# Norms of the gated heads: folding the squares to 64 rows, and one product with ones in place of two

## The chip, the cores and the metric

The kernel runs on one core of one Trainium2 chip. The metric is the device time of one execution in microseconds; lower is better. A run's time is given as the median of several executions, and one execution was recorded by the hardware profiler.

## The reference

One layer of a hybrid decoder trunk, sequence 1024, width 1024, all in float32. Its input is normalized and projected by one wide matrix (7184 columns). Eight heads of differential softmax attention and four heads of gated linear attention (GLA, value width 256) run beside each other, each head's output is normalized and gated, and both are projected back. What matters here is the norm of the gated heads:

```python
def rms_norm(x, g):
    xf = x.astype(jnp.float32)
    y = xf * lax.rsqrt(jnp.mean(xf * xf, axis=-1, keepdims=True) + NORM_EPS)
    return (y * g.astype(jnp.float32)).astype(x.dtype)
...
    ob = gla_chunked(...)                  # (B, S, 4 heads, 256)
    ob = rms_norm(ob, gla_g).astype(x.dtype)
    ob = ob.reshape(B, S, GLA_WIDTH) * jax.nn.silu(gb)
```

So for every position and head, 256 squares have to be summed.

## The kernel before

**Number format.** Products run on TensorE in a reduced form of float32. A value is split into a high part (a rounding copy on ScalarE, `act.copy` into an `F32R` tile) and a low part (value minus high part, a subtraction on VectorE), and three of the four cross products are summed. Line 117, the helper `mm`, issues every matmul, and line 120 (`tr`) every transpose. Both are kept in the order in which the program gives them; the instructions of the other engines, and SP's DMAs, are put in order by a planner that estimates when each would be ready (some are pinned, too).

**The projection.** The wide product is made by a scheme of seven products of half blocks (Strassen's kind) for each pair of 128-column blocks. The list `order` has 196 steps `(pair, n)`. A step is 12 matmuls of 512 columns, or 24 of 256 for most pairs, on results `x`, `y`, `z` in PSUM. `go(n)` runs steps. Before a step, `prepare` makes the weights of that and the three following steps: raw weights (`w_raw`, loaded at line 194), sums of them on VectorE (line 296), high part on ScalarE (315), low part on VectorE (316), in a ring of five tiles. Finished sums (`c`, lines 411 and 440) leave through SP's queue to DRAM, to be loaded again by the heads. For the attention values (kind `VA`, steps 97 to 141 in part) a step `n = 7` takes three tiles of the ring `c`.

**The ring `c`.** `t_c(name)` takes a tile of a ring of four (128 rows, 512 floats). The copies `s` of some steps, the sums `c`, the output weights' high parts `wo_hi`, and the norms' `sq` and `r` all come from it. A tile whose content is stored becomes free when the store has landed.

**The gated heads.** `gla(g)` is a generator; each `yield` ends one portion. The four heads run in a chain, `fill`, of which `go` takes one portion after each projection step from step 86 on:

```python
    go(order.index((12, 5)) - made[0])
    fill.append(chain(*(gla(g) for g in range(GLA_HEADS))))
    go(len(order) - made[0] - LEAD)
    for _ in fill[0] if fill else ():
        pass
```

With `LEAD = 8` there are 102 such steps (86 to 187); what is left of the chain after them would run by itself. A head has two halves of 512 positions. In one half: the loads; `pa` and `pk` (scores in the chunk and transposed keys; GpSimd masks the scores, line 775); `kv` (state updates, `gu` on VectorE); `gpo` (outputs, copied to `go`, the tile `o`); then the norm (lines 826 to 859). The value width of 256 lies in two parts of 128 rows. ScalarE squares both (`sqs`), VectorE adds them (`sq`), and the sum over the 128 rows is a product with a matrix of ones: one matmul with the high part and one with the low part of `sq` (`gms`). Ln and Exp on ScalarE give `r`, then VectorE scales and gates `o`, and high and low parts are stored to `mixe` (line 856). A half takes 11 portions, and three steps lie between the squares and the product.

The attention heads' norms (`attn_norm`, lines 1126 to 1138) sum 128 rows; there the squares are folded to 64 rows, and high and low part share one tile of 128 rows and one product.

**What comes behind.** After step 187 the queries and keys of the first attention head are loaded (`load_qk`, lines 875 and 878) into buffers that the gated heads used: `ks` goes into the tags `ks0` and `ks1`, in which `o` and the gates lie. The scores (`sc`) begin after the last step, with the output product (`ypart`) beside them.

Of the kernel before, what the change touches and what calls it, by code (L numbers as in the profile page):

```python
# [9 lines left out]
F32R = mybir.dt.float32r  # L10
AF = mybir.ActivationFunctionType
ALU = mybir.AluOpType
PSUM = bass.MemoryType.PSUM

P = 128
# [16 lines left out]
def hymba_kernel(  # L32
# [21 lines left out]
    act, dve, pool, pe, sp = nc.scalar, nc.vector, nc.gpsimd, nc.tensor, nc.sync  # L54

    def fp(t):
        return t.bitcast(F32)
# [11 lines left out]
    ones = const.tile([P, P], F32R, name="ones")  # L69
# [40 lines left out]
    def take_bank(shape, name):  # L110
        i = free.pop(0)
        return bank(i, shape, name), i
# [3 lines left out]
    def mm(*a, **k):  # L116
        tc.keep_in_program_order(pe.matmul(*a, **k))  # L117
# [35 lines left out]
    kp = ctx.enter_context(tc.tile_pool(name="kp", bufs=1))  # L153
# [3 lines left out]
    def t2k(tag, bufs, name, dt=F32, shape=(P, 512)):  # L157
        return ap.tile(list(shape), dt, tag=tag, name=name, bufs=bufs)

    def t_c(name, dt=F32):  # L160
        return t2k("c", 4, name, dt)
# [55 lines left out]
    i = order.index((1, 4))  # L217
# [540 lines left out]
    def gla(g):  # L758

        u = None  # L760
        for half in range(2):
# [48 lines left out]
            for m in range(2):  # L810
                po, ib = take_bank([P, 2, 256], "gpo")
                for i in range(2):
                    c = slice((2 * m + i) * P, (2 * m + i + 1) * P)
                    for t in range(2):
# [3 lines left out]
                            start=True, stop=(us[2 * m + i] is None),  # L818
# [9 lines left out]
            sqs = kp.tile([P, 2, 512], F32, tag="k1", name="sqs")  # L828
            for t in range(2):
                act.activation(sqs[:, t], o[:, t], AF.Square)  # L830
            sq = t_c("sq")
            dve.tensor_tensor(sq, sqs[:, 0], sqs[:, 1], ALU.add)
            hl = kp.tile([P, 2, 512], F32R, tag="k1", name="sq_hl")
            act.copy(hl[:, 0], sq)
            dve.tensor_tensor(hl[:, 1], sq, fp(hl[:, 0]), ALU.subtract)
            yield
            yield
            yield
            ms, ib = take_bank([P, 512], "gms")
            for i in range(2):  # L840
                mm(ms, ones, hl[:, i], start=(i == 0), stop=(i == 1))
            r = t_c("r")
            act.activation(r, ms, AF.Ln, bias=eps_t, scale=1.0 / 256)
            free.append(ib)
# [39 lines left out]
# [5 lines that stand above are left out]
# [636 lines left out]
```

## Time and profile before

| what | value |
|---|---|
| time, median of 3 runs | 982.13 us (981.99 to 982.59) |
| profiled execution, its own time | 980.34 us |
| its span, first to last instruction | 978.6 us |
| granted TensorE clock, mean | 0.999 |
| instructions | 15745 |
| projection steps with gated heads beside them | about 278 to 590 us |

A row of the profile names the line, engine, operation, the tile written `<-` the tiles read, the size, and how often it ran. PE is TensorE's matmuls, PEld its weight loads, DVE VectorE, ACT ScalarE, POOL GpSimd, SPq the queue from which SP issues DMAs. Brackets at the end of a row of the timeline hold the time that the engine had been idle before it, and what ended that. A matmul's duration is its latency: successive matmuls overlap, so the distance between starts is what one costs.

### The profile page before, as it was taken

How to read it: one execution, taken by the hardware profiler on the slowest of the kernel's cores; microseconds unless marked ns; L12 is line 12 of the kernel's file. 1: busy time of each engine (PE TensorE's matmuls, PEld its weight loads, DVE VectorE, ACT ScalarE, POOL GpSimd, SP SyncE). 2: the span in 40 equal slices, each digit the busy share in tenths (PEclk: the TensorE clock that was granted, in tenths of full speed). 3: DMA queues.
4: the chain of work that ended last, by engine and by line, in shares of the span. 5: the costliest groups of instructions: out<-in, count | busy, mean ns of one | idle time of the engine just before them, and what ended most of it. 6: DMA issues, size and time to landing. Idle time of an engine off the chain costs nothing.

```text
span 978.6 us, 15745 instructions
## 1 busy us (share of the span) xinstructions
PE 956.6 (98%) x5338; PEld 829.7 (85%) x5338; DVE 736.0 (75%) x1452; ACT 600.9 (61%) x1164; POOL 135.3 (14%) x142
## 2 busy tenths in 40 slices
PE   6999999999999999999999999999999999999997
PEld 5998988888889998899888888878888888888785
DVE  6986597798766677586786876487888888898554
ACT  8642365486467445445566765366777687887773
POOL 4300000000000010000100100021322222443322
PEclk9999999999999999999999999999999999999999
DMA  9443456646765858897988866997657669994777
GB/s 353 143 123 93 124 148 202 229 169 233 253 234 168 266 183 276 247 299 230 298 254 255 270 191 217 357 300 250 206 173 234 233 202 351 351 283 107 151 209 146
DMA packets 152593, 220.45 MB, mean 225 GB/s; under 512 B 17104, under 2 KB 83664, under 8 KB 152416
## 3 DMA queue, kind: packets, MB, share of 16 engines
q1 hardware_dynamic: 148480, 212.10, 66.5%
q0 software_dynamic: 4032, 7.34, 4.8%
q8 instruction: 42, 0.69, 0.3%
q14 instruction: 39, 0.32, 0.1%
HBM read 133.93 MB, written 88.60 MB: 227 GB/s over the span
## 4 chain that ended last, share of the span: by engine, by line
PE 87%; DMA 4%; DVE 4%; ACT 2%; issue 1%; SPq 1%; POOL 0%; DVEq 0%; ACTq 0%; POOLq 0%
PE x L117 21%; PE y L117 14%; PE z L117 14%; PE ypart L117 13%; PE sc L117 7%; PE po L117 5%; PE yps L117 4%; PE wtr L120 3%; PE gpo L117 2%; DMA ks<-k_d 1%; PE kv L117 1%; DMA wo_raw<-in_w_out_dram 1%; DMA w_raw<-in_w_in_dram 1%; PE gkl_ps L117 1%; DVE w L316 1%
## 5 line engine op out<-in xcount | busy, mean ns | idle before, releaser
L315 ACT CAST w<-w_raw 128x512 fp32r<-128x512 f32 (+1 forms) x164 | 112.4, 688 | 97.2 <-PE y L117 46.2
L316 DVE TENSOR_TENSOR w<-w_raw,w 128x512 fp32r<-128x512 f32 (+1 forms) x164 | 126.5, 773 | 52.1 <-ACT w L315 45.6
L1048 ACT ACTIVATE p<-p,stt 128x896 f32<-128x896 f32 (+7 forms) x128 | 99.3, 777 | 37.7 <-DVE stt L1038 33.6
L427 ACT COPY s<-x 128x512 f32<-128x512 f32 x84 | 49.1, 585 | 86.9 <-PE x L117 83.9
L1054 POOL TENSOR_SCALAR p<-p,stt,lam 128x1024 f32<-128x1024 f32 (+3 forms) x64 | 56.2, 877 | 226.2 <-DVE stt L1053 223.8
L296 DVE TENSOR_TENSOR w_raw<-w_raw 128x512 f32<-128x512 f32 (+1 forms) x96 | 75.8, 790 | 15.4 <-DMA w_raw<-in_w_in_dram 14.1
L1038 DVE CUSTOM_DVE_ANT_0 p<-sc,maskt 128x512 f32<-128x512 f32 (+3 forms) x128 | 74.3, 585 | 14.9 <-PE sc L117 13.8
L775 POOL TENSOR_SCALAR_AFFINE_SELECT gan<-gan 128x512 f32<-128x512 f32 x8 | 17.6, 2198 | 486.3 <-ACT gan L774 486.3
L117 PE MATMUL ypart<-wo_hi,m_hi 128*128 128x512 f32 x192 | 79.6, 414 | 0.1
L117 PE MATMUL y<-h_hi,w 128*128 128x512 f32 x320 | 79.6, 391 | 0.0
L117 PE MATMUL z<-s_hi,w 128*128 128x512 f32 x320 | 79.6, 391 | 0.0
L117 PE MATMUL x<-s_hi,w 128*128 128x512 f32 x320 | 79.6, 391 | 0.0
L117 PE MATMUL ypart<-wo_hi,m_lo 128*128 128x512 f32 x192 | 75.5, 393 | 0.0
L117 PE MATMUL ypart<-wo_lo,m_hi 128*128 128x512 f32 x192 | 75.4, 393 | 0.0
L117 PE MATMUL sc<-k,q 128*128 128x512 f32 (+1 forms) x192 | 69.0, 363 | 1.2 <-DVE stt L1038 1.2
L117 PEld LDWEIGHTS x<-s_hi,w 128*128 128x128 f32 x320 | 59.7, 188 | 12.2
L117 PEld LDWEIGHTS y<-h_hi,w 128*128 128x128 f32 x320 | 59.6, 188 | 12.2
L117 PEld LDWEIGHTS z<-s_hi,w 128*128 128x128 f32 x320 | 59.5, 188 | 12.0
L117 PE MATMUL sc<-ks,q 128*128 128x512 f32 (+1 forms) x192 | 66.1, 347 | 1.0 <-DMA ks<-k_d 1.0
L1096 ACT CAST wt_hi<-wtr 128x512 fp32r<-128x512 f32 (+1 forms) x80 | 42.8, 535 | 25.3 <-PE wtr L120 24.5
L1097 DVE TENSOR_TENSOR wt_lo<-wtr,wt_hi 128x512 fp32r<-128x512 f32 (+1 forms) x80 | 50.6, 633 | 9.1 <-ACT wt_hi L1096 8.5
L1057 DVE SCALAR_TENSOR_TENSOR p<-p,stt,p 128x1024 f32<-128x1024 f32 (+3 forms) x64 | 52.1, 814 | 4.1 <-POOL p L1054 3.9
(224 smaller groups left out, 2237.3 us busy)
## 6 DMA issues: line engine op xcount, KB each, us to landing
w_raw<-in_w_in_dram SPq DMA_DIRECT2D x56, 512.0 KB, 4.5
wo_raw<-in_w_out_dram SPq DMA_DIRECT2D x32, 256.0 KB, 2.8
wo_d<-wo_hi SPq DMA_DIRECT2D x32, 256.0 KB, 2.9
wo_d<-wo_raw SPq DMA_DIRECT2D x32, 256.0 KB, 3.3
q<-q_d SPq DMA_DIRECT2D x32, 256.0 KB, 4.6
k<-k_d SPq DMA_DIRECT2D x32, 256.0 KB, 5.3
ks<-k_d SPq DMA_DIRECT2D x64, 128.0 KB, 6.5
wo_hi<-wo_d SPq DMA_DIRECT2D x16, 512.0 KB, 6.4
```

Source lines behind the costliest of these rows:

```text
L117: tc.keep_in_program_order(pe.matmul(*a, **k))
L120: tc.keep_in_program_order(pe.transpose(dst, src, ident))
L296: dve.tensor_tensor(dst, a, b, ALU.subtract)
L315: act.copy(w[0], src)
L316: dve.tensor_tensor(w[1], src, fp(w[0]), ALU.subtract)
L427: act.copy(b[k], ps)
L1038: ins = dve.tensor_tensor_reduce(p[:, a:e], sc[:, : e - a], maskt[:, NZ + P - (e - a) :] if last else maskt[:, : e - a], 1.0, 3e38 if i == ...
L1048: act.activation(p[:, :n], p[:, :n], AF.Exp, bias=st[:, m : m + 1], scale=-1.0, accum_out=st[:, 2 + m : 3 + m],)
L1054: pool.tensor_scalar(p1[:, :n], p1[:, :n], st[:, 5:6], lam, ALU.mult, ALU.mult)
L1057: dve.scalar_tensor_tensor(p0[:, :n], p0[:, :n], st[:, 4:5], p1[:, :n], ALU.mult, ALU.subtract)
L1096: act.copy(hi[:, :n], pt[:, :n])
L1097: dve.tensor_tensor(lo[:, :n], pt[:, :n], fp(hi[:, :n]), ALU.subtract)
```

## The change

The two parts' squares are added as before, but for rows 0 to 63 and rows 64 to 127 separately (`sq` and `fold`, both in rows 0 to 63 of a tile of the ring `c`), and a third addition folds the two into 64 rows. The high part of these goes into rows 0 to 63 of `sq_hl` and the low part into rows 64 to 127, so that one product with ones sums both. One `yield` more stands between the squares and the product, so a half takes 12 portions.

```diff
             sqs = kp.tile([P, 2, 512], F32, tag="k1", name="sqs")
             for t in range(2):
                 act.activation(sqs[:, t], o[:, t], AF.Square)
-            sq = t_c("sq")
-            dve.tensor_tensor(sq, sqs[:, 0], sqs[:, 1], ALU.add)
-            hl = kp.tile([P, 2, 512], F32R, tag="k1", name="sq_hl")
-            act.copy(hl[:, 0], sq)
-            dve.tensor_tensor(hl[:, 1], sq, fp(hl[:, 0]), ALU.subtract)
+            sq, fold = t_c("sq")[:64], t_c("fold")[:64]
+            dve.tensor_tensor(sq, sqs[:64, 0], sqs[:64, 1], ALU.add)
+            dve.tensor_tensor(fold, sqs[64:, 0], sqs[64:, 1], ALU.add)
+            dve.tensor_tensor(sq, sq, fold, ALU.add)
+            hl = kp.tile([P, 512], F32R, tag="k1", name="sq_hl")
+            act.copy(hl[:64], sq)
+            dve.tensor_tensor(hl[64:], sq, fp(hl[:64]), ALU.subtract)
+            yield
             yield
             yield
             yield
             ms, ib = take_bank([P, 512], "gms")
-            for i in range(2):
-                mm(ms, ones, hl[:, i], start=(i == 0), stop=(i == 1))
+            mm(ms, ones, hl, start=True, stop=True)
             r = t_c("r")
             act.activation(r, ms, AF.Ln, bias=eps_t, scale=1.0 / 256)
             free.append(ib)
```

## The prediction

> **What bounds the kernel now.** I read the page's engine shares and chain first, then the windows around the gated heads, then what TensorE waited for in them. The page's lines:
>
> ```profile
> span 978.6 us, 15745 instructions
> PE 956.6 (98%) x5338; PEld 829.7 (85%) x5338; DVE 736.0 (75%) x1452; ACT 600.9 (61%) x1164; POOL 135.3 (14%) x142
> PE 87%; DMA 4%; DVE 4%; ACT 2%; issue 1%; SPq 1%; POOL 0%; DVEq 0%; ACTq 0%; POOLq 0%
> ```
>
> TensorE is busy for 956.6 of 978.6 us and is 87% of the chain that ended last. That is an average, so I cut out the stretch in which the gated heads run (278 to 590 us). Columns: the stretch and its length, then busy time (instructions) of PE, PEld, DVE, ACT and POOL, the granted clock, DMA share and GB/s.
>
> ```profile
> 278.00:340.00 62.00, 62.00 (x418) 57.15 (x416) 39.76 (x57) 37.59 (x64) 1.73 (x2) 1.00 0.68 219
> 340.00:420.00 80.00, 79.18 (x520) 72.32 (x519) 54.85 (x84) 40.14 (x69) 5.07 (x2) 1.00 0.76 237
> 420.00:590.00 170.00, 170.00 (x977) 149.72 (x976) 127.41 (x201) 103.26 (x184) 10.79 (x4) 1.00 0.81 255
> 590.00:640.00 50.00, 49.90 (x221) 41.06 (x220) 29.36 (x53) 23.49 (x40) 0.50 (x1) 1.00 0.82 290
> ```
>
> In these 312 us TensorE is idle for 0.82 us, at the full clock. VectorE is busy for 39.76 + 54.85 + 127.41 = 222.0 us (71%), ScalarE less. So a product taken out here shortens the stretch by its slot, as long as TensorE keeps finding its next operands ready. What TensorE waited for, in the stretch (first two lines) and after 590 us (us in total, times, longest):
>
> ```profile
> PE gpo L117 <- DVE gu L803: 0.5, 1, 0.5
> PE kv L117 <- DVE c L411: 0.3, 1, 0.3
> PE sc L117 <- DVE stt L1038: 1.2, 2, 0.9
> PE sc L117 <- DMA ks<-k_d: 1.0, 1, 1.0
> ```
>
> Neither wait of the stretch is for the norms' product `gms`: making its operands is already hidden. Moving it later therefore removes no wait of its own.
>
> **The products that go.** Each of the eight halves (four heads, two halves of the sequence) issued two products with ones; one is left. The timeline around one pair, and the group:
>
> ```profile
> 381.25 1.98 PE L117 MATMUL x<-h_hi,w 128*128 128x512 f32 x8
> 383.07 1.07 PE L117 MATMUL x<-h_lo,w 128*128 128x512 f32 x4
> 383.97 0.62 PE L117 MATMUL gms<-sq_hl,ones 128*128 128x512 f32 x2
> 384.43 2.00 PE L117 MATMUL y<-h_hi,w 128*128 128x512 f32 x8
> L117 PE MATMUL gms<-sq_hl,ones x16: 388/392/397, 307.9 to 570.7; 128*128 128x512 f32 x16
> ```
>
> The 392 ns are latency; matmuls overlap. What counts is the distance between starts: (383.97 − 381.25)/12 = 0.227 us, and (384.43 − 383.97)/2 = 0.23 us for the pair itself. I take 8 × 0.227 = 1.82 us off TensorE. The remaining product is as wide (512 columns) and as deep (128 rows) as each of the old ones, so it costs one slot. Eight loads of ones go as well, which ran under the products.
>
> [...]
>
> **What is added on VectorE.** Before, each half had an add and a subtraction over 128 rows; after, three adds and a subtraction over 64 rows. The attention heads' norms have such 64-row operations already (ns min/median/max):
>
> ```profile
> L832 DVE TENSOR_TENSOR sq<-sqs x8: 682/689/694, 299.1 to 561.7; 128x512 f32<-128x512 f32 x8
> L1128 DVE TENSOR_TENSOR sq<-sq,fold x16: 673/678/684, 684.1 to 933.3; 64x512 f32<-64x512 f32 x16
> L1130 DVE TENSOR_TENSOR sq_hl<-sq,sq_hl x16: 684/685/1572, 686.5 to 934.7; 64x512 fp32r<-64x512 f32 x16
> ```
>
> Half the rows take the same time: 678 against 689 ns. So two operations more per half are 2 × 0.68 = 1.36 us, and 16 of them 10.9 us, which brings VectorE in the stretch from 222 to 233 of about 310 us (75%). ScalarE's two squares and its rounding copy cost what they cost. All of it lies beside TensorE. The cover at one half is this:
>
> ```profile
> 376.72 0.69 DVE L832 TENSOR_TENSOR sq<-sqs 128x512 f32<-128x512 f32 x1 [0.92 <-ACT sqs L830]
> 378.15 0.69 DVE L835 TENSOR_TENSOR sq_hl<-sq,sq_hl 128x512 fp32r<-128x512 f32 x1 [0.74 <-ACT sq_hl L834]
> ```
>
> The low part is ready at 378.84, the product starts at 383.97: 5.1 us of slack. The two operations take 1.4 of it, the additional step gives 12 × 0.227 = 2.72 back, so about 6.4 us remain and `gms` does not wait. If that cover were gone, each further microsecond would be TensorE's.
>
> [...]
>
> ```profile
> 356.52 0.68 DVE L854 TENSOR_TENSOR go<-go,gg 128x512 fp32r<-128x512 f32 x1
> 357.12 0.69 DVE L413 TENSOR_TENSOR c<-c,v_hi 128x512 fp32r<-128x512 f32 x1
> 357.73 1.72 DVE L296 TENSOR_TENSOR w_raw<-w_raw 128x512 f32<-128x512 f32 x2
> ```
>
> Neighbours start 0.60 us apart at a duration of 0.68, so an overlap is worth 0.08 us. [...]
>
> **What is moved.** A half takes 12 steps in place of 11: eight halves take 96 of the 102 that are there (steps 86 to 187), so nothing is left over to run bare. Within a half only the distance from the squares to the product grows. But each later half meets the projection steps one, two, … seven steps later, the last `gms` 8 × 2.72 = 21.8 us later. Everything behind it moves along: `r`, the gating, four stores to `mixe`, then on SP's queue the `ks` loads of the first attention head, which wait for those buffers.
>
> ```profile
> 577.03 0.37 SPq L856 DMA_DIRECT2D mixe<-gg  x1
> 580.05 0.41 SPq L856 DMA_DIRECT2D mixe<-go  x1
> 581.18 1.81 SPq L878 DMA_DIRECT2D ks<-k_d  x3
> 589.14 0.51 SPq L878 DMA_DIRECT2D ks<-k_d  x1
> 632.55 0.40 PE L117 MATMUL sc<-k,q 128*128 128x512 f32 x1
> DMA to landing us min/median/max: 3.2/6.5/8.6
> ```
>
> The last `ks` load goes from 589.1 to about 611, among the output weights' loads, and lands by 620 at the longest landing. The first scores would then start at 630.7. 11 us remain, so I cost this move at nothing; beyond them it would cost microsecond for microsecond.
>
> The two waits of the stretch also depend on what meets what:
>
> ```profile
> 362.59 0.69 DVE L411 TENSOR_TENSOR c<-y,s 128x512 f32<-128x512 f32 x1 [3.13 <-DMA v_d<-c]
> 363.33 1.16 PE L117 MATMUL kv<-gv,gan 128*128 128x128 f32 x8 [0.28 <-DVE c L411]
> 408.31 1.23 DVE L296 TENSOR_TENSOR w_raw<-w_raw 128x1024 f32<-128x1024 f32 x1 [2.35 <-DMA w_raw<-in_w_in_dram]
> 409.45 0.47 DVE L803 SCALAR_TENSOR_TENSOR gu<-gu,dstep,kv 128x256 f32<-128x256 f32 x1
> 409.98 0.49 PE L117 MATMUL gpo<-gqd,gu 128*128 128x128 f32 x2 [0.55 <-DVE gu L803]
> ```
>
> At 362.59 VectorE stood 3.13 us because a slot of the ring `c` (four) was held by a store, and the `kv` products lost 0.28 us. At 408.31 it stood 2.35 us for raw weights, and the state update behind that made `gpo` lose 0.55 us. After the change this `kv` comes two projection steps later and this `gpo` three, so both meetings break up (−0.83 us); new ones can form, with the same kinds of waits. Bounds: all 0.83 goes and none comes, or it goes and more comes (below). I take half of it as gained, 0.4, because the same traffic is still there.
>
> **The sum.** −1.82 − 0.4 = −2.2 us. The profiled execution took 980.34 us (1.74 around the span) and would take 978.1. It is 1.79 us under the median of the runs, so I subtract from the median: 982.13 − 2.2 = 979.9 us.
>
> **The rivals.**
>
> *The slot is saved, but new meetings take their share.* The planner orders the other engines by its own estimates, and 16 VectorE operations more shift them. With between 0.7 and 4.6 us of waits in the stretch in place of 0.83 the time stays within 0.2% (1.96 us), which is about what a measurement of this kernel can tell from no change. One more wait like `gpo`'s beside the old 0.83 gives 982.13 − 1.82 + 0.55 = 980.9. For it: two such waits exist already. Against: only two in eight halves.
>
> *The ring `c` runs out (slower).* `sq` and `fold` hold two of its four slots at once, so a half takes three tiles of it and not two. In the second half of the first head, `r` was taken after step 107, ahead of the value pair's steps 108 and 109, which take six; now it is taken after step 109, behind them. The landing that frees a slot:
>
> ```profile
> v_d<-c SPq DMA_DIRECT2D x32, 128.0 KB, 3.5
> ```
>
> There VectorE's wait of 3.13 us already used up TensorE's cover to 0.28. If one more landing (3.5) and the two additional operations (1.2 at their spacing of 0.60) come on top, TensorE loses 4.7 us more: 982.13 − 1.82 + 4.7 = 985.0. It decides from 3.8 us of new waits on. For it: that place and its wait are in the trace. Against: `sq` and `fold` are both gone before step 108, and the six other halves meet emptier steps.
>
> *The end of the gated heads comes too late (slower).* If the `ks` loads were held on SP's queue for 11 us beyond their shift, the scores would wait; 15 us of hold would give 982.13 − 1.82 + 4 = 984.3. Nothing there shows it.
>
> That the change does not do what it says I don't expect: the 64 rows of high parts and 64 of low parts stack to 128, which ones sum in one product.
>
> **How the numbers follow.** Forecast (fewer waits in the stretch than before, by 0.14 us or more): 0.47. New meetings eat the margin: 0.30. Ring or late end: 0.23, nearly all the ring. Fast end of the range: 1.82, the 0.83 of waits and the 1.0 us wait for `ks` all gone, 978.5. Slow end: the ring at one place, 985.0. The forecast's own range is 978.5 to 980.2. Chances: faster 0.47, same 0.30, slower 0.23.
>
> **What would show it.** Right: `gms` eight times in place of 16; TensorE 5330 matmuls and 954.8 us busy; VectorE 1468 instructions and about 747 us; the last `gms` near 590 us, the last `mixe` store near 601, the first `sc` near 630.5; no wait of `gms` for `sq_hl`; no `kv` wait near 363 and no `gpo` wait near 409. Wrong: TensorE waits in the gated stretch above 0.83 us, led by `c`, `s` or `w` behind a store's landing, or a wait of `sc` for `ks` above 1.0 us.

## The result and the profile after

The change made the kernel slower: 994.05 us in the median of 6 runs (990.77 to 998.15) against 982.06 us of the kernel before on the same chip (981.42 to 982.81, 6 runs). The ratio is 1.0127, 95% interval 1.0102 to 1.0153. The forecast was 979.9 us with a range of 978.5 to 985.0: the sign was wrong and the result lies outside the range. The profiled execution took 990.77 us, the shortest of the six, so the trace shows a mild case: 10.4 us more than the profiled execution before (980.34).

The page of the changed kernel, the lines that answer to the first ones of the prediction:

```profile
span 989.1 us, 15766 instructions
PE 959.9 (97%) x5330; PEld 831.5 (84%) x5330; DVE 745.5 (75%) x1468; ACT 602.7 (61%) x1164; POOL 126.5 (13%) x142
PE 84%; DMA 7%; DVE 4%; ACT 2%; issue 1%; SPq 1%; POOL 0%; DVEq 0%; ACTq 0%; POOLq 0%
```

The counts are those forecast (5330 matmuls, 1468 VectorE instructions), and 7% of the chain is now DMA in place of 4%. TensorE is busy for 5 us more than the forecast 954.8, with fewer matmuls. The windows say where. Columns as in the prediction; the changed kernel first, then the kernel before in the two stretches that differ:

```profile
420.00:590.00 170.00, 168.44 (x968) 147.80 (x967) 125.86 (x201) 101.58 (x181) 5.54 (x4) 1.00 0.76 239
620.00:640.00 20.00, 16.46 (x66) 13.02 (x65) 8.89 (x15) 4.82 (x8) 0.00 (x0) 0.91 0.94 306
640.00:660.00 20.00, 16.18 (x72) 12.46 (x71) 15.25 (x47) 11.71 (x24) 4.91 (x5) 1.00 0.89 288
660.00:700.00 40.00, 38.15 (x194) 32.10 (x195) 28.29 (x81) 22.78 (x52) 6.79 (x9) 0.96 0.81 241
```

```profile
620.00:640.00 20.00, 19.90 (x89) 16.21 (x88) 12.82 (x27) 8.18 (x13) 0.50 (x1) 1.00 0.97 329
640.00:660.00 20.00, 17.76 (x90) 14.12 (x89) 16.63 (x52) 12.51 (x33) 5.67 (x7) 1.00 0.94 297
```

Beside the gated heads (278 to 590 us) TensorE idles 1.56 us in place of 0.82. From 620 to 700 us, where the projection gives way to attention, it idles 9.2 us in place of 2.3, and the granted clock falls to 0.91 and 0.96. Idle time in that transition (+6.9), idle time in the gated stretch (+0.7) and busy time (959.9 − 956.6 = +3.3) make 10.9 us; the span grew by 10.5.

What TensorE waited for (us in total, times, longest):

```profile
PE ypart L117 <- DVE c L363: 2.5, 1, 2.5
PE ypart L117 <- DMA m_lo<-mixe: 2.4, 2, 1.4
PE ypart L117 <- DMA m_hi<-mixe: 1.9, 1, 1.9
PE x L117 <- ACT s L427: 1.6, 2, 0.8
```

The two waits of before (`kv`, `gpo`) are gone, as forecast, and no `gms` waits for `sq_hl`. New are three kinds of waits of the output product `ypart`. Its start in the timeline:

```profile
633.23 0.47 PE L117 MATMUL ypart<-wo_hi,m_hi 128*128 128x512 f32 x1 [2.55 <-DVE c L363]
634.70 0.79 PE L117 MATMUL ypart<-wo_hi,m_lo 128*128 128x512 f32 x1 [1.00 <-DMA m_lo<-mixe]
...
636.15 0.63 PE L117 MATMUL ypart<-wo_hi,m_lo 128*128 128x512 f32 x1
636.58 0.63 PE L117 MATMUL ypart<-wo_lo,m_hi 128*128 128x512 f32 x1
...
639.60 0.39 PE L117 MATMUL sc<-k,q 128*128 128x512 f32 x1
639.83 0.39 PE L117 MATMUL sc<-ks,q 128*128 128x512 f32 x1
```

The same start in the kernel before, without a wait:

```profile
630.80 0.39 PE L117 MATMUL ypart<-wo_hi,m_hi 128*128 128x512 f32 x1
```

Behind the waits the matmuls start 0.43 us apart, a few microseconds later 0.23 apart: TensorE runs at about half speed for a while (granted clock 0.52 from 634.7 to 637.8 us). By the granted clock of the windows this is (1 − 0.91) × 20 + (1 − 0.96) × 40 = 3.4 us, the larger part of the 5 us of busy time too many; what the rest is stays open. SP's queue, first of the changed kernel, then of the kernel before:

```profile
617.25 6.70 SPq L880 DMA_DIRECT2D ks<-k_d  x8
...
625.63 0.38 SPq L928 DMA_DIRECT2D m_hi<-mixe  x1
626.10 0.40 SPq L928 DMA_DIRECT2D m_lo<-mixe  x1
```

```profile
618.22 0.32 SPq L926 DMA_DIRECT2D m_hi<-mixe  x1
619.02 0.32 SPq L926 DMA_DIRECT2D m_lo<-mixe  x1
```

Before, the eight `ks` loads were issued at 581 to 589 us. Now they stand at 617 to 624, for 6.7 us, ahead of three loads of output weights and of `m_hi` and `m_lo`, which `ypart` reads; these go 7 us later.

The profile puts the first wait of `ypart`, 2.55 us, to VectorE's `c` at line 363. That operation ended at 632.80. But `m_hi`, issued at 625.63, took 7.5 us to land, so it was there at 633.1, and the matmul starts at 633.23. So `m_hi` ended this wait as well. `m_lo`, issued at 626.10, landed 8.6 us later, at 634.7, where the second wait ends. In the kernel before, `m_hi` had landed at 624.7 (6.5 us after its issue), 6 us ahead of the first `ypart`. The other two waits, 1.92 us at 658.86 and 1.37 us at 660.69, are for the next `m_hi` and `m_lo`.

### The profile page after: what moved, and what is told of

Its sections match the earlier page's. It is cut to its first block, busy times and chain, and to the rows that moved or that the text cites. A ratio compares the mean times of both kernels' runs of the same rounds, so it can differ in the third digit from the quotient of the medians.

```text
span 989.1 us, 15766 instructions
## 1 busy us (share of the span) xinstructions
PE 959.9 (97%) x5330; PEld 831.5 (84%) x5330; DVE 745.5 (75%) x1468; ACT 602.7 (61%) x1164; POOL 126.5 (13%) x142
## 4 chain that ended last, share of the span: by engine, by line
PE 84%; DMA 7%; DVE 4%; ACT 2%; issue 1%; SPq 1%; POOL 0%; DVEq 0%; ACTq 0%; POOLq 0%
PE x L117 21%; PE y L117 13%; PE ypart L117 13%; PE z L117 13%; PE sc L117 7%; PE po L117 5%; PE yps L117 4%; PE wtr L120 3%; PE gpo L117 2%; DMA wo_d<-wo_raw 2%; DMA ks<-k_d 2%; PE kv L117 1%; DMA m_lo<-mixe 1%; PE gkl_ps L117 1%; DVE w L316 1%
## 5 line engine op out<-in xcount | busy, mean ns | idle before, releaser
L775 POOL TENSOR_SCALAR_AFFINE_SELECT gan<-gan 128x512 f32<-128x512 f32 x8 | 9.0, 1130 | 511.6 <-ACT gan L774 476.8
```

## The experiments

Times are medians, each beside the kernel before on the same chip. The idle columns are worked out from the profiled execution: 312 or 80 us less TensorE's busy time in the window. That is one execution, and in some runs it lies off the median: it took 997.73 us in run 3 and 988.50 in run 4 (the longest there), 984.21 in run 15, and 979.15 in run 17.

| kernel | time, us | before there | ratio (95%) | idle 278–590 | idle 620–700 |
|---|---|---|---|---|---|
| before | – | – | – | 0.82 | 2.34 |
| after | 994.05 | 982.06 | 1.0127 (1.0102–1.0153) | 1.56 | 9.21 |
| 1 fold only | 986.14 | 982.27 | 1.0038 (1.0015–1.0061) | 6.53 | 2.42 |
| 2 step only | 1002.80 | 982.27 | 1.0206 (1.0188–1.0223) | 7.30 | 8.72 |
| 3 ks behind mix | 995.10 | 982.27 | 1.0128 (1.0094–1.0162) | 6.19 | 9.06 |
| 4 step in two heads | 984.49 | 982.27 | 1.0031 (1.0012–1.0050) | 6.04 | 2.35 |
| 5 ks late alone | 987.20 | 980.91 | 1.0059 (1.0044–1.0075) | 1.37 | 5.73 |
| 6 length kept | 991.73 | 980.91 | 1.0121 (1.0102–1.0139) | 8.37 | 2.81 |
| 7 fold, wo on GpSimd | 991.27 | 980.91 | 1.0095 (1.0076–1.0114) | 7.92 | 2.17 |
| 8 before, wo on GpSimd | 983.16 | 980.91 | 1.0021 (1.0011–1.0032) | 0.95 | 1.34 |
| 9 step where tight | 986.65 | 981.48 | 1.0059 (1.0037–1.0080) | 8.11 | 2.23 |
| 10 late end alone | 991.64 | 981.48 | 1.0105 (1.0089–1.0121) | 0.67 | 7.15 |
| 11 fold, no wo load | 979.45 | 981.47 | 0.9969 (0.9956–0.9982) | 2.10 | 2.52 |
| 12 tight, no wo load | 978.05 | 981.47 | 0.9968 (0.9952–0.9983) | 0.95 | 1.84 |
| 13 before, no wo load | 979.56 | 980.86 | 0.9986 (0.9972–1.0000) | 0.00 | 2.39 |
| 14 before, early wo load | 980.04 | 980.86 | 0.9993 (0.9983–1.0003) | 0.00 | 3.40 |
| 15 tight, early wo load | 981.43 | 980.86 | 1.0010 (1.0000–1.0021) | 4.54 | 1.84 |
| 16 fold, early wo load | 981.35 | 980.86 | 1.0011 (0.9998–1.0023) | 2.56 | 2.94 |
| 17 step in three, early | 980.54 | 981.13 | 0.9998 (0.9982–1.0014) | 1.29 | 2.04 |
| 18 whole change, early | 990.42 | 981.13 | 1.0086 (1.0065–1.0107) | 1.71 | 7.13 |

The two idle columns fall apart into two separate losses. The rest of this section takes them one after the other, after the first four runs, which split the change.

### Splitting the change (1 to 4)

**1, fold only**: the changed kernel without its additional `yield`.

> The fold and the single product, without the additional step (11 portions per half, 88 in all). Theory Q (queue): the loss comes from the eight later steps alone, because the last half's stores and with them the eight ks loads land on SP's queue right ahead of the first loads of mixe (m_hi, m_lo). Without the step the ks loads are issued before 592 us, m_hi near 617, the first ypart does not wait, and the time is 979 to 981 us (1.8 us of products and up to 0.8 us of old waits gone). Rival V (VectorE and ring c): the 16 more operations and 8 more tiles cost the time in the gated stretch; then this kernel is slower than 984 us, like the whole change.

Q's 979 to 981 was missed: 986.14. The transition is as before, but the gated stretch now has 6.5 us of idle time, most of it where the prediction saw none:

```profile
PE gms L117 <- DVE sq_hl L837: 3.8, 2, 2.3
```

**2, step only**: the kernel before with the additional `yield`, no fold.

> The kernel before with the additional step only: two products per half, squares over 128 rows, 12 portions per half. Theory Q: as slow as the whole change or slower by the eight products kept, 992 to 1000 us, with m_hi issued after 624 us and over 2 us of waits at the first ypart. Rival V: no fold, so within 1.5 us of 982.

1002.80, worse than the whole change: the step alone brings the late end (8.7 us idle from 620 to 700) and 7.3 us in the gated stretch, two waits of 3.4 and 3.3 us of `x` for `s` among them.

**3, ks behind mix**: the whole change, with the `ks` loads of the first head issued in the program behind `mix0 = mix(0)`.

> The whole change, but the ks loads of the first attention head are issued with, and not ahead of, the first mixe loads (they are written behind mix(0) in the program). Nothing else is moved. Theory Q: m_hi and m_lo are issued some 6 us earlier (near 619 us) and the first ypart waits under 0.5 us; the ks loads, issued to about 627 us, land near 634, so the first sc may wait 1 to 3 us; time 981 to 987 us. Rival V: no change, 992 to 998 us. Rival T (total traffic: 88 MB more or less beside each other, not the order): no change either.

Missed: 995.10. Six of the eight `ks` loads now went behind `m_hi`, two still ahead of it. The first `m_hi` landed in time (at 637.1, the first `ypart` started at 637.94). But the next `m_hi` was issued at 661.1, 23 us behind that start, where it had been 13 us in the kernel before, and TensorE waited 5.6 us for it. So putting the first `m_hi` ahead did not save the time: the queue was late behind it.

**4, step in two heads**: the whole change, with the step only in the first two heads (`if g < 2: yield`), so the end comes four steps later and not eight.

> The whole change, but the additional step only in the first two heads (92 portions): the last half ends four steps later than before and not eight. Theory Q, with a threshold: the ks loads go out before the first output weights (about 602 us), so nothing is lost and the time is 979 to 981.5 us. If instead the loss grows with each step of delay, half of it stands, 986 to 989 us. Rival V: 990 us or more, since every fold is there.

The transition is like before (2.35 us): four steps of shift cost nothing there, and eight some 10 us, as run 10 will show. But 6.0 us of idle time stay in the gated stretch, a single `gms` wait of 3.5 us among them, so the time, 984.49, fits neither figure.

### The late end (5 and 10)

**5, ks late alone**: no fold, no step; in the kernel before, the first head's `ks` loads are pinned behind the output weights' loads.

```diff
-    for n in ("q", "k", "ks"):
+    for n in ("q", "k"):
         load_qk(0, n, 1)
...
+    for half in (1, 0):
+        load_qk(0, "ks", half)
     mix0 = mix(0)
```

> The kernel before with one edit: the eight ks loads of attention head 0 stay behind the output weights' loads on SP's queue, just ahead of the first m_hi (where the changed kernel has them), although their buffers come free at 581 us as before. No fold, no additional step. Theory H (the end of the gated heads costs time because 1 MB of ks loads moves from a gap at 581 to 589 us into the full stretch of transfers at 610 to 640): the first m_hi is issued near 625 in place of 618, ypart, sc and ks waits appear, the time is 988 to 993. Rival L (the cost comes from the late stores to mixe and the late gating, not from the ks loads): 981.5 to 984.

Between the two, nearer to H's 988 than to L's 984: 987.20, 6.3 us above the kernel before. SP's queue and the place where it was paid:

```profile
619.01 6.86 SPq L878 DMA_DIRECT2D ks<-k_d  x8
625.97 0.53 SPq L928 DMA_DIRECT2D m_hi<-mixe  x1
...
656.77 0.76 PE L117 MATMUL ypart<-wo_hi,m_hi 128*128 128x512 f32 x1 [3.74 <-DMA m_hi<-mixe]
```

`m_hi` is issued at 625.97 in place of 618.22, as in the changed kernel. It landed 4.1 us later, at 630.1, ahead of the first `ypart` at 631.43; but everything behind it on the queue is late, and the next `m_hi`, issued at 650.07 in place of 644.14, costs 3.74 us.

**10, late end alone**: the kernel before, with eight more portions ahead of the last half's norm product.

```diff
+            for _ in range(8 if 2 * g + half == 7 else 0):
+                yield
```

> The kernel before with eight additional steps ahead of the last half's norm product only: no fold, all other halves where they were, TensorE's order the same but for that one pair of products. The end of the gated heads comes 21.8 us later. Theory E (the late end is the whole of the changed kernel's loss in the transition, some 10 us, of which the ks loads alone gave 6): 990 to 994, with ypart waits for m_hi and m_lo, the gated stretch idle as before (under 1.2 us). Rival K (the ks loads are all of it, the rest comes from the shifts of the other halves): 985 to 988.

991.64, 10.2 us more, as theory E had it, with a gated stretch that idles 0.67 us. The waits are those of the changed kernel:

```profile
PE ypart L117 <- DMA m_lo<-mixe: 2.6, 2, 1.3
PE ypart L117 <- issue: 1.8, 1, 1.8
...
PE ypart L117 <- DMA m_hi<-mixe: 0.9, 1, 0.9
```

The wait that the profile puts to `issue` ends with `m_hi` again: issued at 626.58, it landed 6.7 us later, at 633.3, and the matmul starts at 633.37. So the late end by itself is some 10 of the 12 us, and the late `ks` loads by themselves some 6 of these. What the remaining 4 are made of (the late stores to `mixe`, the later `q` and `k` loads, the half-speed matmuls behind the first wait) was not taken apart.

### The gated stretch (6 to 9)

**6, length kept**: the whole change, with the `yield` behind the gate buffer's request taken out, so that a half has 11 portions.

> The whole change, with the step taken away that stood between the request of a half's gate buffer and its first product pa: a half has 11 portions as before, the norm's product still comes one step later behind the squares. Theory (two separate costs: the chain of the fold in the gated stretch without its step, and the late end with it): neither is met; the transition is like before (no ypart wait), TensorE idles 0.5 to 2 us in the gated stretch, 980 to 982.5. Rival (the place of each half against the projection steps decides, by chance): TensorE idles 4 to 7 us in the gated stretch, as with the fold alone and with the step in two heads, 984 to 987.

The end is early again, but 991.73: 8.4 us idle in the gated stretch. Its largest wait also shows what a wait drags behind it:

```profile
537.58 3.78 PE L117 MATMUL z<-s_hi,w 128*128 128x512 f32 x8 [3.36 <-DVE c L440]
541.16 1.91 PE L117 MATMUL z<-s_lo,w 128*128 128x512 f32 x4
```

Eight matmuls take 541.16 − 537.58 = 3.58 us, 0.45 each, after 3.36 us of waiting.

I then read the slack at all eight halves of the kernel before (start of `gms` less the end of the low part): 5.5, 7.3, 5.1, 2.3, 2.0, 2.5, 1.4 and 6.0 us. Two of the tight ones:

```profile
419.21 0.68 DVE L835 TENSOR_TENSOR sq_hl<-sq,sq_hl 128x512 fp32r<-128x512 f32 x1
422.14 0.62 PE L117 MATMUL gms<-sq_hl,ones 128*128 128x512 f32 x2
...
531.66 0.69 DVE L835 TENSOR_TENSOR sq_hl<-sq,sq_hl 128x512 fp32r<-128x512 f32 x1 [1.94 <-ACT sq_hl L834]
533.77 0.62 PE L117 MATMUL gms<-sq_hl,ones 128*128 128x512 f32 x2
```

**7, fold with the output weight's preparation on GpSimd**, and **8**, the same in the kernel before:

```diff
-            act.copy(hi, raw)
+            pool.tensor_copy(hi, raw)
             lo = raw.bitcast(F32R)
-            dve.tensor_tensor(lo, raw, fp(hi), ALU.subtract)
+            pool.tensor_tensor(lo, raw, fp(hi), ALU.subtract)
```

> The fold alone (no additional step), and the output weight's preparation (its rounding copy wo_hi from ScalarE, its subtraction from VectorE) moved to GpSimd, so that neither engine stands in its queue for the landing of wo_raw. Theory W (ScalarE's and VectorE's stand at wo_hi for the load of wo_raw is what the fold's chain meets): the gms waits for sq_hl and the x waits for s in the gated stretch go, TensorE idles below 2 us there, 980 to 982.5. [...]

> The kernel before with only the output weight's preparation moved to GpSimd: what that move does by itself. Theory W: the stretch had 0.83 us of waits, so at most that is gained, 981 to 982.5. Rival (GpSimd's work slows VectorE, or its masks a<-a come late behind wo_raw's load and gpo waits): 984 or more.

Theory W failed in this form: 991.27, worse than the fold alone, `gms` still waits 4.2 us. Rows of VectorE and TensorE of run 7 at the half around 420 us, and one of VectorE's waits:

```profile
419.06 1.23 DVE L296 TENSOR_TENSOR w_raw<-w_raw 128x1024 f32<-128x1024 f32 x1 [4.50 <-DMA w_raw<-in_w_in_dram]
420.20 0.68 DVE L832 TENSOR_TENSOR sq<-sqs 64x512 f32<-64x512 f32 x1
...
425.22 0.68 DVE L837 TENSOR_TENSOR sq_hl<-sq,sq_hl 64x512 fp32r<-64x512 f32 x1
425.96 0.59 PE L117 MATMUL gms<-sq_hl,ones 128*128 128x512 f32 x1 [2.11 <-DVE sq_hl L837]
```

```profile
DVE fold L833 <- DMA wo_d<-wo_hi: 4.4, 2, 3.2
```

The squares had been written by 416.1. VectorE reached them at 420.20, because an addition of raw weights stood in front of them for 4.5 us until its load had landed. And where the stand for `wo_raw` was taken off ScalarE, `wo_hi` kept its slot of the ring `c` instead, and VectorE's `fold` waited for that. The wait had moved, not gone. Run 8 (983.16, +2.3 us) lies between its two figures and says that GpSimd's part costs something by itself.

**9, step where tight**: the whole change, with the step only in halves 3 to 6.

```diff
+            if 3 <= 2 * g + half < 7:
+                yield
```

> The fold in all halves, the additional step only in halves 3 to 6 (counted from 0): those whose low part was ready only 2.3, 2.0, 2.5 and 1.4 us ahead of the norm's product before the change (the other four had 5 to 7 us). The end comes four steps later, not eight. Theory S (the slack of each half decides whether gms waits, and four steps of shift cost nothing at the end): no gms wait for sq_hl, TensorE idles 0.5 to 2.5 us in the gated stretch, the transition is like before: 980 to 983. Rival M (every shift of the halves makes new meetings with late loads, whatever the slack): TensorE idles 4 to 7 us in the stretch, through s and c copies behind a load's landing, 984 to 988.

Half of each theory. No `gms` waits any more, as S had it, and the transition is like before. But `x` waits 6.5 us for `s`, as M had it, and `kv` 1.6 us for the ring `c`: 8.1 us of idle time, above what either theory gave, and 986.65. SP, ScalarE and TensorE at the first of the two large ones:

```profile
494.11 0.53 SPq L592 DMA_DIRECT2D wo_raw<-in_w_out_dram  x1
...
497.48 0.62 ACT L584 CAST wo_hi<-wo_raw 128x512 fp32r<-128x512 f32 x1 [4.67 <-DMA wo_raw<-in_w_out_dram]
...
500.22 0.57 ACT L427 COPY s<-x 128x512 f32<-128x512 f32 x1
500.83 2.11 PE L117 MATMUL x<-s_hi,w 128*128 128x512 f32 x8 [2.14 <-ACT s L427]
```

ScalarE stood 4.67 us for a piece of the output weight that had been asked for only 3.4 us earlier; behind it came the copies of `go` (498.01), the squares (499.16), and the copy `s` (500.22), for whose bank TensorE waited. The products of `x` that `s` copies had ended at 495.98, and ScalarE ran without a pause from 497.48 on, so `s` stood for the work ahead of it on ScalarE and not for its operand.

### The loads of `wo_raw` (11 to 18)

`wo_raw` has a single buffer, and the low part was written over it; so each load waits for the store of the piece before. In runs 11 to 13 the loads are left out; in 14 to 18 they are all there, but free of that wait and one step earlier:

```diff
-            lo = raw.bitcast(F32R)
+            lo = t_st("wo_lo", F32R)
...
-        if n in (2, 4) and wo_todo:
+        if n in (1, 6) and wo_todo:
```

**11 and 12**, the fold alone and the fold with the step where slack was tight, and **13**, the kernel before:

> The fold alone, with the loads of wo_raw left out: the output weight's high and low parts are made, as often and on the same engines, from a tile that is in place (so its output is not the reference's), and stored as before. Neither ScalarE nor VectorE can stand for that load, and 8 MB less come in between the projection steps. Theory W2 (what the fold's chain meets in the gated stretch is mostly the stand at wo_hi behind its load, on ScalarE and through it on VectorE): TensorE idles under 2.5 us from 278 to 590 us, where the fold alone has 6.5; no gms wait over 0.5; the time 978 to 982. Rival R (it is the loads of w_raw and the stores that hold the ring c): TensorE idles 4 to 7 us there, 983 to 987.

> As the run with the step in halves 3 to 6 only, with the loads of wo_raw left out in the same way (the output is not the reference's). Theory W2: its 6.5 us of x waits for s fall to under 2, TensorE idles under 2 us from 278 to 590 us (8.1 with the loads), 977 to 981. Rival R: two of the four x waits stay, TensorE idles 4 to 8 us there, 982 to 987.

> The kernel before with the loads of wo_raw left out, as in the two runs ahead (the output is not the reference's): the control to them. If leaving the loads out helps only what the fold meets, this one stays within 1 us of the kernel before, 980.5 to 982.5, and the fold without those loads is 1 to 3 us faster than it. If the loads cost the kernel before as well, 977 to 980, and the fold gains nothing even then.

W2 was right: 6.5 us of idle time fell to 2.1 (with one `gms` wait of 1.0 us, more than it allowed), and 8.1 to 0.95. The control without the loads came to 979.56, 1.3 us under the kernel before, so by its figures the loads cost the kernel before something too. Run 12 stands at 0.9968 of the kernel before and the control at 0.9986; the difference is 1.8 us, the size of the products' saving, but the intervals overlap, so this points to the saving and doesn't show it. TensorE's busy time agrees with it: 954.7 us in run 12, 956.8 in run 13.

**14**, the kernel before, **15**, the fold with the step where tight, and **16**, the fold alone, all with the earlier loads:

> The kernel before, with the output weight's low part written to the ring st in place of over wo_raw, so that wo_raw comes free when VectorE has read it and not when a store has landed; its next load is issued in the same step, one earlier than before (nothing is left out). Theory W3 (the stand for wo_raw's landing is what the shifted halves meet; the kernel before meets little of it): 980.5 to 982.5. Rival (32 more tiles in the ring st make their own waits): 983 to 986.

> The fold with the step in halves 3 to 6, with the same earlier loads of wo_raw (complete, nothing left out). Theory W3: TensorE idles under 3 us in the gated stretch (8.1 with the late loads, 0.95 without any), 978.5 to 981.5, faster than the kernel before by 0.5 to 3 us. Rival: the ring st or w_raw takes over, idle 4 to 8 us, 983 to 987.

> The fold alone, no additional step, with the same earlier loads of wo_raw (complete). Theory W3: some gms wait is left, as without any load (2.1 us idle in the stretch), 979 to 982. Rival: gms waits of 3 us and more, 983 to 987.

With the traffic kept, the fold alone comes from 986.14 to 981.35 and run 9's kernel from 986.65 to 981.43, while the kernel before hardly moves (980.04 against 980.86; 980.5 to 982.5 was expected). The fold's idle time falls from 6.53 to 2.56 us, nearly to the 2.10 without any load. So it is the stand for this load, not the traffic, that most of the shifted work met. The edit also moves the loads to other steps and the low part to another ring; that this is not just one more shift rests on the agreement with runs 11 and 12. ScalarE's waits from 278 to 600 us, run 1 and run 16:

```profile
ACT wo_hi L584 <- DMA wo_raw<-in_w_out_dram: 30.9, 11, 5.3
```

```profile
ACT wo_hi L584 <- DMA wo_raw<-in_w_out_dram: 7.3, 7, 2.7
```

The same copies have other waits in run 16, which the profile puts to other transfers (4.8 and 2.0 us) or to nothing (0.6), so they stood for 14.7 us in all, half of run 1's 30.9.

Run 16 came out as W3 had it, and run 15 inside W3's range of times. Yet neither is faster than the kernel before, as W3 wanted of run 15: run 15, whose profiled execution (984.21 us) was the longest of its twelve, has one `x` wait of 2.5 us in it, more idle time than W3 allowed; run 16 keeps a `kv` wait of 1.3 us and a `gms` wait of 1.1, 2.4 us in all against the 1.8 saved.

**17**, the earlier loads with the step in halves 0, 1 and 3, and **18**, the earlier loads in the whole change:

> The fold with the earlier loads of wo_raw, and the additional step in halves 0, 1 and 3 only: the first two move the next head's state update away from the value pair whose store holds the ring c (the kv wait of 1.3 us at 365), the third covers the half whose norm product still waited 1.1 us. The end comes three steps later. If the two waits left behind the early loads are all that stands between the fold and its 1.8 us: TensorE idles under 1 us in the gated stretch, 978.5 to 980.5, about 1 to 2 us faster than the kernel before. If each shift makes new meetings: idle 2 to 5 us, 981 to 984.

> The whole change, all eight steps, with the earlier loads of wo_raw. If the two losses are separate, the late end stays although the gated stretch is mended: idle under 2 us from 278 to 590 us, the ypart waits for m_hi and m_lo as in the changed kernel, 989 to 993. If the stand for wo_raw also made the late end: 980 to 984.

Run 17 is the best full version with the fold: 980.54 against 981.13, ratio 0.9998 (0.9982 to 1.0014), no difference that can be told. It lies between its two figures: the `kv` wait is gone, but one `gms` wait of 1.3 us is there. Run 18 shows the two losses to be separate: a gated stretch with 1.71 us of idle time, and the late end as it was:

```profile
PE ypart L117 <- issue: 3.2, 1, 3.2
PE ypart L117 <- DMA m_lo<-mixe: 1.3, 2, 0.7
```

Here too the wait put to `issue` ends when `m_hi` lands (issued at 627.29, landed 7.1 us later; the matmul starts at 634.45). Against its own kernel before it loses 9.3 us where the changed kernel lost 12.0; its four runs lie within 2.2 us, the changed kernel's six within 7.4. That the wider spread comes from stands for `wo_raw`, which differ from run to run, fits this but wasn't profiled.

## Why the prediction was wrong, point by point

- **"I cost this move at nothing" failed, and with it the sign.** The step looked only at when `ks` must land for the scores. The first scores did not wait for `ks`, as it had it (the 0.6 us wait of `sc` comes later, at 670). But the last `ks` load went at 623 and not at about 611: the last store to `mixe`, issued at 605.4, took 7.7 us to land, and stores of `q` went out ahead of the loads. And the step didn't ask what stands behind the `ks` loads on SP's queue. These are `m_hi` and `m_lo`, which `ypart` reads ahead of the scores, in a stretch whose DMA share is 0.94 (0.97 before). `m_hi` landed at 633.1 in place of 624.7, `ypart` waited for it, and the first scores came at 637.0 in place of the forecast 630.5. Late `ks` loads alone cost 6 us (run 5), the late end as a whole 10 (run 10).
- **The third rival was this mechanism in part, with the wrong price and chance.** It had SP's queue held and the scores waiting, 984.3, with hardly any chance, because nothing in the trace before showed it. The rows were there: `m_hi` at 618 us and output weights' loads from 602 on, at a DMA share of 0.82 from 590 to 640 us. The cost doesn't grow evenly with the shift: four steps cost nothing there (run 4), eight cost 10 us; nothing between was run.
- **"About 6.4 us remain and `gms` does not wait" was right for the changed kernel and wrong as an argument.** The slack was read at one half of eight; four others had 1.4 to 2.5 us. And two operations of 0.68 us don't lengthen the chain by 1.4: around 420 us it took 5.1 us from the squares to the low part before (414.78 to 419.89) and 7.8 in run 1 (418.57 to 426.36), since other work and the stands in VectorE's queue lie between its parts. The additional step covered this: no `gms` wait in the changed kernel, 3.8 us without the step. The step's own price of 2.72 us was right; it is that of 12 matmuls of 512 columns, the form of 140 of the 196 steps (56 have 24 of 256, so that form is the rarer one). The spacing on VectorE was a little wider than the 0.60 us that the prediction read at 356 to 358 us: the fold's first two operations start 0.72 us apart (299.76 and 300.48), so 0.12 us more; the starts at 301.20 and 306.22 come 0.72 and 0.71 us behind the ones before, and the three make only 0.35 us in this half.
- **The meetings: right in kind, too small.** The old `kv` and `gpo` waits broke up as forecast, and the profiled execution has 1.6 us of `x` waits in their place. But the runs with other shifts of the halves found new ones: 6.0 to 8.4 us of idle time in runs 1 to 4, 6 and 9, where the first rival allowed up to 4.6. I had named `c`, `s` and `w` behind a store's landing; most of it was the single buffer of `wo_raw`, whose late load holds ScalarE's and VectorE's queues, a thing that the trace before shows (24.0 us of ScalarE's idle time from 278 to 600 us, and 17.6 us of VectorE's behind the same copies) and that cost at most 0.8 us of TensorE's time there, by the luck of the places.
- **The ring `c`** wasn't what decided: the `kv` wait behind a store of the ring grew from 0.28 to 1.6 us in run 1 and is absent in the changed kernel. The 3 to 4.7 us of the second rival were too much for that place.
- **The saving** has the size that was worked out, as far as it can be seen: TensorE's busy time is 954.7 us in run 12 (954.8 forecast), though 959.9 in the changed kernel, where the half-speed stretches come on top. VectorE's 745.5 us (747 forecast) and the last `gms` at 592 (590) were close; the last store to `mixe` came at 605, 4 us later than forecast.

## What to carry to other kernels

Slack that hides added work has to be read at every repetition, and the path through an engine's queue counts with all that stands between its links (in run 9, 4.67 us for a load ahead of the copy `s`). When a stage ends later, list what its last transfers release, what then stands behind those on the DMA queue, and who reads that first; the price need not grow evenly with the shift, as the four and the eight steps here show. A load into a single buffer, read by an engine that others depend on, can cost time after a later change of timing, even where it costs next to nothing today. And where a profile's label of a wait names an operation that ended early, look up when the operands' loads landed.

## What the hardware showed that I had not expected

- After 2.55 and 1.00 us of waiting (the changed kernel at 633 us) matmuls of 512 columns start 0.43 us apart in place of 0.23, until 637.8; after 1.92 and 1.37 us (at 659 to 661) they come to 0.43 apart as well, and after 3.36 us (run 6) to 0.45. This comes on top of the wait: seven matmuls from 634.70 to 637.77 took 3.07 us in place of 1.6, and 13 in run 6, from 537.58 to 543.29, 5.71 us in place of 2.95. Ahead of the stretch at 634.7 TensorE had stood for 3.55 us in two pieces, with one matmul between, and ahead of that in run 6 for 3.36 us in one.
- The block of `ks` loads on the queue is longer in the changed kernel (6.7 us) than the four blocks before (4.5 us in all), but the single issue is not: 0.44 to 0.61 us before, 0.44 to 0.60 after. The eight add up to 4.2 us; in the other 2.5 us the queue stood between them, by the profile for landings of the output weights' loads.
